# A fused decoder trunk on one core: gathered expert sums enter the output by products with 0-1 matrices, and the last three V tiles are used whole

## The chip, the cores and the metric

One core of a Trainium2 chip. The metric is the device time of one launch in microseconds (us), the median of several runs.

## The reference

Four residual layers over 256 tokens of width 1024, all in float32: an attention and retention mixer, a PEER layer, a short-convolution mixer ("odd mixer"), a second PEER layer, and a final RMSNorm. The change lies in the two PEER layers and in what follows each:

```
def peer(xn, w_q, sub_keys, u, v):        # 16384 experts, 8 heads, top 16: 128 experts for a token
    ...                                   # scores, top-k, gate (softmax), eidx
    hid = gelu(einsum('td,thkd->thk', tc, u[ec]))
    return einsum('thk,thkd->td', gc * hid, v[ec])

h = h + peer(rmsnorm(h, norm_ffn[layer]), ...)
...
return rmsnorm(h, final_norm)
```

## The kernel before

**Two ways through PEER.** The first 96 tokens (`TG`) are *gathered*: for each of 96 steps a row of `u`, later of `v`, is fetched for each of 128 partitions by an indirect transfer of 512 KB on GpSimd's queue. Partitions 0 to 95 hold one token each, with 96 of its 128 experts; partitions 96 to 127 work off the other 32 experts of tokens 0 to 31, then 32 to 63, then 64 to 95 (`SUB` = 32). The other 160 tokens (`TD`) are *dense*: all of `u` and `v` stream through as 128 tiles of 512 KB each (the U stage and the V stage), by eight buffers (`RAW`), on the queues of SyncE and, for odd V tiles, ScalarE.

**The V stage.** Eight PSUM tiles `vo[b]`, one for 128 of the 1024 output columns, hold the output transposed (columns on partitions, tokens along the free axis). Tiles in `SPL` are split: ScalarE rounds the tile to `vhi` (L1415), VectorE forms the bf16 rest `vlo` (L1422); the hidden values are split likewise (`row_parts`, `row_rest`, L1486 to L1494), and TensorE takes a product of 320 columns (L1539) and one of 160 (L1541) for each b. The other tiles are used whole, in a float32 product of 160 columns (L1504). `carry` does the splitting three tiles ahead, so that it stands that early in the instruction streams.

**The gather in the V stage.** `ga.step()` is called for every tile and adds `ga.rate` to a credit; each whole credit consumes one fetched row (`consume`, L1038: acc = row x weight + acc on VectorE) and issues the next row into the freed one of six buffers. The own tokens' sum runs on from `acc[0]` to `acc[2]`; the partial sums of partitions 96 to 127 start anew at each third and are copied by `part` (L1049, 128 KB) to the tokens' partitions of `acc[0]`. After the last step two folds (L1045) add `acc[2]` and `acc[0]` to the residual `h`. The rate is set so that the last step falls at tile 121.

**The last blocks.** `END` = 3 tiles are kept for the end, where the loop over b is outside: TensorE finishes block b for all three tiles, then ScalarE copies it out of PSUM (L1555), VectorE adds the second half of the split products (L1556), and the next norm's operand is formed. In layer 0 (`Folded`) a product with the identity puts h of the gathered tokens into the block first (L1566); the operand `x2` of the odd mixer is scaled by ScalarE and VectorE (L538, L539), and `st.parts()` splits the mixer's weight tiles 0 and 1 into the buffers `hi` and `lo`, at the start and at block 3. In layer 1 (`Final`) `fetched` normalises the gathered tokens' rows on its own and sends them out (L587 to L598); the blocks hold the dense tokens alone, squares and scaled blocks are formed (L625, L626), transposed back (L637), and scaled by the root (L663 to L669).

**The streams.** All is emitted in a written order (a manual schedule), one in-order stream for each engine. `hi` and `lo` have three buffers each, used by U's prefetch, V's splits and the mixers' splits in turn; in the mixers `st.deep` names the tiles that take two further ones. The odd mixer reads its weights in threes per k: the first pair at L280, the others at L263.

Of the kernel before, what the change touches and what calls it, by code (L numbers as in the profile page):

```python
# [15 lines left out]
OP = mybir.AluOpType  # L16
# [30 lines left out]
SPL = [i for i in range(NK) if i % 2 or i % 4 == 0 and i > 0]  # L47
# [6 lines left out]
END = 3  # L54
# [8 lines left out]
C_N = C_ONE + 1  # L63
# [7 lines left out]
def shape_constants():  # L71
# [3 lines left out]
    c[:, C_ONE] = 1.0  # L75
    c[:, C_ST:C_ST + TK] = np.array(STARTS)[None, :]
# [29 lines left out]
class Stream:  # L106
# [31 lines left out]
    def _split(self):  # L138
# [5 lines left out]
        pools = self.more if i < self.end and (self.end - i) % 5 in self.deeper else (self.hi_pool, self.lo_pool)  # L144
# [52 lines left out]
def trunk_kernel(ctx, tc, x, small, cst, mcst, ew_in, ew_out, ow_in, ow_out, wq, keys, pu, pv, pun, gains, out):  # L197
# [139 lines left out]
    Z = pers.tile([P, S], BF16, tag="z", name="z")  # L337
# [175 lines left out]
    class Folded(Norm):  # L513


        def begin(self, XT, fold):

            st.parts()
            new_x2()
            self.XT = XT  # L520
            self.fq = {}
            self.fold = fold

        def block(self, b, pend):
# [4 lines left out]
            if b == 3:  # L529
                st.parts()  # L530
# [42 lines left out]
    class Final(Sums):  # L573
# [4 lines left out]
        def __init__(self, g):  # L578
            super().__init__()
            self.g = g  # L580
            self.junk = Xb.rearrange("p k t -> p (k t)")[:, :512]

        def warm(self):
            nc.sync.dma_start(self.g, gains[2])
            self.table()

        def fetched(self):  # L587

            rows = slice(0, TG)
            for ch in range(2):  # L590
                act.activation(self.junk, h[:, 0, ch * 512:(ch + 1) * 512], AF.Square,
                               accum_out=self.w[:, 0, ch:ch + 1])
            self.mean0(0)
            self.root(0)
            self.rstd(0)
            v.scalar_tensor_tensor(h[rows, 0, :], h[rows, 0, :], self.scale(0)[rows], self.g[rows],
                                   op0=OP.mult, op1=OP.mult)
            nc.sync.dma_start(out[0, rows, :], h[rows, 0, :])  # L598

        def begin(self, XT, fold):  # L600
# [9 lines left out]
            v.memset(self.GX[:, :, :TG], 0.0)  # L610
            v.memset(self.SQ, 1.0)
# [8 lines left out]
        def ready(self, b):  # L620

            xt = self.XT[:, b, TG:]
            gain = G[:, 7 * ND + b:7 * ND + b + 1]
            sq = self.SQ[:, 1 if b else 0, TG:]
            act.activation(sq, xt, AF.Square)  # L625
            v.tensor_scalar(self.GX[:, b, TG:], xt, gain, None, op0=OP.mult)  # L626
# [1009 lines left out]
```

## Time and profile before

| | |
|---|---|
| median of 3 runs | 1510.13 us (1510.12 to 1511.16) |
| the profiled execution | 1510.24 us, span 1508.4 us |
| TensorE busy | 1442.8 us, 96% |
| VectorE, ScalarE, GpSimd busy | 1255.6, 762.1, 726.3 us |
| moved by DMA | 533 MB, mean 353 GB/s |
| granted TensorE clock, mean | 0.99 |

The span runs from the first to the last instruction; the profiled execution's time has 1.8 us around it. Times in rows count from the span's start. V's stages end near 749 us (layer 0) and 1490 us (layer 1). Idle time of an engine is of interest only where others wait for it, so what is read below are stretches, and who waits for whom at their ends.

### The profile page before, as it was taken

The numbers are of one execution on the slowest core, as the hardware profiler recorded it, in microseconds if no ns is written. First come the engines' busy times: TensorE is split into PE (matmuls) and PEld (weight loads), VectorE is DVE, ScalarE is ACT, GpSimd is POOL, SyncE is SP. The second block draws the span as 40 slices with busy tenths as digits, with TensorE's granted clock in tenths as the row PEclk, the third lists the DMA queues.
The fourth block names the chain that finished last, engine by engine and source line by source line (L and its number), as shares of the span: only waits on it lengthen the run. The fifth ranks groups of instructions, "written<-read, shape, count | busy, mean of one in ns | idle before, by whom it ended". The sixth has DMA issues, their size and how long they took to land.

```text
span 1508.4 us, 30116 instructions
## 1 busy us (share of the span) xinstructions
PE 1442.8 (96%) x11180; PEld 1338.8 (89%) x11180; DVE 1255.6 (83%) x2480; ACT 762.1 (51%) x1821; POOL 726.3 (48%) x514
## 2 busy tenths in 40 slices
PE   9999999999999999989899999999999999998896
PEld 5667999999999998888789799999999999988885
DVE  5637999879998888888866599996999978888887
ACT  5556512268875444444553462113888744444444
POOL 6754545446675343444145373453666724444430
PEclk9999999999999999999999999999999999999997
DMA  8646899999999999999956488999999999999993
GB/s 317 197 153 205 292 401 409 396 409 403 407 403 408 404 401 409 408 399 409 362 189 190 166 294 327 408 408 396 408 405 405 403 397 400 408 408 399 409 408 114
DMA packets 147442, 533.00 MB, mean 353 GB/s; under 512 B 16992, under 2 KB 17248, under 8 KB 147296
## 3 DMA queue, kind: packets, MB, share of 16 engines
q1 hardware_dynamic: 71872, 258.11, 45.6%
q0 software_dynamic: 56704, 205.07, 34.5%
q10 hardware_dynamic: 18720, 67.90, 11.4%
q8 instruction: 88, 1.44, 0.4%
q14 instruction: 58, 0.48, 0.1%
HBM read 528.34 MB, written 1.05 MB: 351 GB/s over the span
## 4 chain that ended last, share of the span: by engine, by line
PE 53%; DMA 29%; DVE 9%; issue 5%; ACT 3%; POOL 1%; ACTq 0%; SPq 0%; DVEq 0%; POOLq 0%
PE hid L1404 28%; DMA raw<-pv 18%; PE hid L263 4%; PE vo L1539 3%; DMA raw<-pu 2%; DMA rows<-pv,ig 2%; PE hid L269 2%; PE vo L1504 2%; DMA rows<-pun,ig 2%; PE G L1364 2%; PE ea L297 2%; PE ea L296 2%; PE ea L295 2%; DMA grow<-pun,ig 2%; DVE vlo L1422 1%
## 5 line engine op out<-in xcount | busy, mean ns | idle before, releaser
L1404 PE MATMUL hid<-xf,raw 128*128 128x160 f32 x3392 | 486.3, 301 | 7.2 <-DMA raw<-pu 4.5
L1404 PEld LDWEIGHTS hid<-xf,raw 128*128 128x128 f32 x3392 | 466.9, 191 | 9.6 <-issue 5.3
L1415 ACT CAST vhi<-raw 128x1024 fp32r<-128x1024 f32 x190 | 198.6, 1045 | 271.0 <-DMA raw<-pv 211.3
L1539 PE MATMUL vo<-ko,vhi 128*128 128x320 f32 x1488 | 265.9, 321 | 31.5 <-DVE ko L1494 31.2
L1422 DVE TENSOR_TENSOR vlo<-raw,vhi 128x1024 bf16<-128x1024 f32 x190 | 231.9, 1222 | 76.2 <-ACT vhi L1415 70.8
L1013 POOL DMA_INDIRECT rows<-pv,ig x128 | 184.6, 1442 | 207.6 <-DVE gacc L1038 173.6
L1539 PEld LDWEIGHTS vo<-ko,vhi 128*128 128x128 f32 x1488 | 220.6, 189 | 40.5 <-DVE ko L1494 40.1
L1013 POOL DMA_INDIRECT rows<-pun,ig x128 | 169.7, 1326 | 135.6 <-DVE rows L1023 63.6
L149 POOL TENSOR_TENSOR lo<-raw,hi 128x1024 bf16<-128x1024 f32 x70 | 168.0, 2413 | 82.5 <-ACT hi L147 78.8
L1023 DVE SCALAR_TENSOR_TENSOR rows<-rows,xg 128x1024 f32<-128x1024 f32 x128 | 155.0, 1216 | 21.5 <-DMA rows<-pun,ig 21.3
L1437 ACT ACTIVATE hg<-hid 128x160 f32<-128x160 f32 (+14 forms) x240 | 62.7, 264 | 216.9 <-PE hid L1404 214.5
L1038 DVE SCALAR_TENSOR_TENSOR gacc<-rows,ghid,gacc 128x1024 f32<-128x1024 f32 x124 | 158.4, 1278 | 5.2 <-DMA rows<-pv,ig 4.7
L1504 PE MATMUL vo<-hg,raw 128*128 128x160 f32 x1056 | 161.7, 304 | 0.7 <-DVE hg L1440 0.7
L1504 PEld LDWEIGHTS vo<-hg,raw 128*128 128x128 f32 x1056 | 147.5, 192 | 1.1 <-DVE hg L1440 1.0
L1013 POOL DMA_INDIRECT grow<-pv,ig x64 | 92.7, 1448 | 113.7 <-DVE gacc L1038 94.3
L1541 PE MATMUL vo<-hb,vlo 128*128 128x160 bf16 x1488 | 135.8, 234 | 0.0
L1013 POOL DMA_INDIRECT grow<-pun,ig x64 | 80.9, 1264 | 77.5 <-DVE grow L1023 44.0
L1354 ACT ACTIVATE ko<-ko,idxT 128x128 f16<-128x128 f16 x320 | 101.6, 391 | 29.3 <-DVE ko L1340 29.1
L1541 PEld LDWEIGHTS <-vlo 128*128 128x128 bf16 x1488 | 98.8, 98 | 19.2 <-DVE vlo L1422 0.3
L147 ACT CAST hi<-raw 128x1024 fp32r<-128x1024 f32 x100 | 102.5, 1047 | 20.2 <-issue 10.1
L263 PE MATMUL hid<-x,hi 128*128 128x256 f32 x800 | 108.5, 289 | 3.5 <-DVE cg L954 2.5
L263 PEld LDWEIGHTS hid<-x,hi 128*128 128x128 f32 x800 | 99.6, 192 | 4.4 <-ACT hi L147 2.7
(264 smaller groups left out, 2136.3 us busy)
## 6 DMA issues: line engine op xcount, KB each, us to landing
raw<-pu SPq DMA_DIRECT2D x212, 512.0 KB, 8.0
raw<-pv SPq DMA_DIRECT2D x128, 512.0 KB, 8.9
raw<-pv ACTq DMA_DIRECT2D x128, 512.0 KB, 8.6
raw<-wq SPq DMA_DIRECT2D x32, 512.0 KB, 4.1
raw<-ew_in SPq DMA_DIRECT2D x28, 512.0 KB, 4.7
raw<-ow_in SPq DMA_DIRECT2D x24, 512.0 KB, 4.5
hg<-pu SPq DMA_DIRECT2D x22, 512.0 KB, 5.5
raw<-ew_out SPq DMA_DIRECT2D x8, 512.0 KB, 3.6
```

Of the source, the lines that this page charges most:

```text
L147: self.nc.scalar.copy(hi, t)
L149: eng.tensor_tensor(lo, t, hi.bitcast(F32), OP.subtract)
L263: pe.matmul(ps[:, :S], hi[:, k * P:(k + 1) * P], A2[:, k, s_, :], start=k == 0 and s_ == 0, stop=False)
L1013: gp.indirect_dma_start(self.row(s_), None, table, bass.IndirectOffsetOnAxis(IG[:, 0, s_ % STEPS:s_ % STEPS + 1].bitcast(U32), 0))
L1023: v.scalar_tensor_tensor(r, r, 1.0, XG[:, q % 2, :], op0=OP.mult, op1=OP.mult, accum_out=w)
L1038: v.scalar_tensor_tensor(self.acc[q], r, w, self.acc[q], op0=OP.mult, op1=OP.add)
L1404: pe.matmul(ps[:, :TD], w[k], XF[:, k, :], start=k == 0, stop=k == ND - 1)
L1415: act.copy(whi[j], raw)
L1422: v.tensor_tensor(wlo[j], raw, whi[j].bitcast(F32), OP.subtract)
L1504: pe.matmul(vo[b][:, TG:S], w[:, c], HG[:, i, :], stop=i == NK - 1, **m)
L1539: pe.matmul(vo[b][:, TG:S + TD], hi[:, b * P:(b + 1) * P], hs, **m)
L1541: pe.matmul(vo[b][:, TG:S], lo[:, b * P:(b + 1) * P], hb, **m)
```

## The change

Each third of the gather now begins its accumulator anew for all 128 partitions (`acc[q]`, no copies, no folds). The sums leave by TensorE: `leave(b, q)` multiplies block b of `acc[q]` with a constant 128 x 96 matrix of zeros and ones (`C_M`, in the constants), which puts a token's own sum and the sum of the partition that helped it into the same column of `vo[b]`. The sets for q = 0 and 1 follow two steps after their third, inside the V loop; the set for q = 2 opens each of the last blocks. The identity products take all 128 tokens of h's first half (before 32). V tiles 125 to 127 are whole. The gather's rate divides by 2 tiles more, so that the last step falls at tile 123. In layer 1 the gathered tokens pass through the last blocks like the others: 256 columns there, no norm of their own, no gains loaded, and all output leaves at the end by four transfers of 256 KB on SyncE's queue. In layer 0 the odd mixer's tiles 0 and 1 are split ahead of the last blocks and tile 2 at block 5, and other tiles of the mixer take the further buffers. The warm-up operand `Z` lies in `Xb` instead of a tile of its own.

The diff, cut:

```
+END = 3
+SPL = [i for i in range(NK - END) if i % 2 or i % 4 == 0 and i > 0]
...
+C_N = C_M + 3 * TG
...
+    for q in range(3):
+        for t in range(TG):
+            c[t, C_M + q * TG + t] = 1.0
+            if t // SUB == q:
+                c[TG + t % SUB, C_M + q * TG + t] = 1.0
...
-    Z = pers.tile([P, S], BF16, tag="z", name="z")
+    Z = Xb[:, 0, :]
...
         def begin(self, XT, fold):                      # Folded; the first st.parts() stays
+            st.parts()
...
-            if b == 3:
+            if b == 5:
                 st.parts()
...
         def warm(self):                                 # Final
-            nc.sync.dma_start(self.g, gains[2])
             self.table()
-        def fetched(self):
...
-            xt = self.XT[:, b, TG:]
+            xt = self.XT[:, b, :]
...
+            for n, (th, ch) in enumerate(((1, 0), (1, 1), (0, 0), (0, 1))):
+                o = self.put[:, ch] if th else h[:, 0, ch * 512:(ch + 1) * 512]
...
+                nc.sync.dma_start(out[th, :, ch * 512:(ch + 1) * 512], o)
...
-            st.deep(mp2, 4 * ND, (1, 2))
+            st.deep(mp2, 4 * ND, [4 * ND - k for k in (3, 4, 8, 9, 13, 14, 19, 20, 25, 26, 30, 31)])
...
-            elif j == 0:
-                v.tensor_scalar(self.acc[0], r, w, None, op0=OP.mult)
             elif j % SUB == 0:
-                v.scalar_tensor_tensor(self.acc[q][:TG], r[:TG], w[:TG], self.acc[q - 1][:TG], op0=OP.mult, op1=OP.add)
-                v.tensor_scalar(self.acc[q][TG:], r[TG:], w[TG:], None, op0=OP.mult)
-                self.part(q - 1)
+                v.tensor_scalar(self.acc[q], r, w, None, op0=OP.mult)
...
-            ga.rate = (ga.TOTAL - ga.c) / (NK - 8.5)
+            ga.rate = (ga.TOTAL - ga.c) / (NK - 6.5)
...
+            def leave(b, q):
+                pe.matmul(vo[b][:, :TG], ga.acc[q][:, b * P:(b + 1) * P], C[:, C_M + q * TG:C_M + (q + 1) * TG],
+                          start=False, stop=False, skip_group_check=True)
...
-                    pe.matmul(vo[b][:, TG:P], h[:, 0, c], ident[:, TG:], **m)
+                    pe.matmul(vo[b][:, :P], h[:, 0, c], ident, **m)
...
-                if i == NK - 6:
-                    assert ga.c == ga.TOTAL
-                    ga.fold(2)
-                if i == NK - 5:
-                    ga.fold(0)
-                if i == NK - 4 and last:
-                    norm.fetched()
+                while sent < 2 and ga.c > STEPS + (sent + 1) * SUB + 1:
+                    for b in range(ND):
+                        leave(b, sent)
+                    sent += 1
...
             for b in range(ND):
-                if not last:
-                    pe.matmul(vo[b][:, :TG], h[:, 0, b * P:(b + 1) * P], ident[:, :TG], start=False, stop=False,
-                              skip_group_check=True)
+                leave(b, 2)
                 for n, w in enumerate(ws):
                     products(b, NK - END + n, w)
```

How the instructions move is shown at three places. First TensorE's first last block in layer 0 (`vo` the block, `h` the residual, `gacc` the accumulator, `ko` and `vhi` the rounded, `hb` and `vlo` the low parts, `hg` and `raw` the whole ones), before:

```order
L1541 LDWEIGHTS vlo_7576
L1541 MATMUL vo_4966<-hb_7528,vlo_7576 128x160
L1566 MATMUL vo_4959<-cst,h 128x96
L1507 MATMUL vo_4959<-ko_4967,vhi_7574 128x320
L1508 LDWEIGHTS vlo_7589
L1508 MATMUL vo_4959<-hb_7528,vlo_7589 128x160
L1504 MATMUL vo_4959<-hg_1256,raw_7507 128x160
L1507 MATMUL vo_4959<-ko_4967,vhi_7610 128x320
L1508 LDWEIGHTS vlo_7633
L1508 MATMUL vo_4959<-hb_7612,vlo_7633 128x160
```

and now:

```order
L1517 MATMUL vo_4965<-hb_7538,vlo_7583 128x160
L1493 MATMUL vo_4958<-cst,gacc_1259 128x96
L1475 MATMUL vo_4958<-hg_1255,raw_7504 128x160
L1475 MATMUL vo_4958<-hg_1255,raw_7517 128x160
L1475 MATMUL vo_4958<-hg_1255,raw_7541 128x160
L1493 MATMUL vo_4959<-cst,gacc_1259 128x96
```

The first product of a block reads the accumulator instead of h, and three whole products stand where five of both kinds stood.

Second, VectorE at the end of layer 1's V stage (`nw` the norm's small columns, `fin` the last blocks' tile), before, where rows of the small norm chain are left out between the two pieces:

```order
L1038 SCALAR_TENSOR_TENSOR gacc_8857<-rows_9645,ghid_8858,gacc_8857 128x1024
L1422 TENSOR_TENSOR vlo_15172<-raw_15068,vhi_15147 128x1024
L1045 TENSOR_TENSOR h<-gacc_8857,h 96x1024
L1422 TENSOR_TENSOR vlo_15183<-raw_15092,vhi_15170 128x1024
L1045 TENSOR_TENSOR h<-gacc_8855,h 96x1024
```

```order
L596 SCALAR_TENSOR_TENSOR h<-h,nw_8849,xf 96x1024
L1422 TENSOR_TENSOR vlo_15234<-raw_15129,vhi_15202 128x1024
L1494 TENSOR_TENSOR ko_12560<-hg_8853,ko_12560 128x160
L610 MEMSET fin_15237 128x8x96
L611 MEMSET fin_15237 128x512
```

and now:

```order
L1393 TENSOR_TENSOR vlo_15139<-raw_15035,vhi_15113 128x1024
L1465 TENSOR_TENSOR ko_12540<-hg_8833,ko_12540 128x2x160
L1018 SCALAR_TENSOR_TENSOR gacc_8837<-rows_9625,ghid_8838,gacc_8837 128x1024
L1393 TENSOR_TENSOR vlo_15159<-raw_15059,vhi_15137 128x1024
L1018 SCALAR_TENSOR_TENSOR gacc_8837<-rows_9625,ghid_8838,gacc_8837 128x1024
L1529 TENSOR_TENSOR xg<-vo_12532,xg 128x160
L611 TENSOR_SCALAR fin_15202<-xg,small 128x256
L1529 TENSOR_TENSOR xg<-vo_12533,xg 128x160
```

Between the last accumulation and the first block's add nothing is left; the last accumulation itself now stands behind the low half of tile 124 instead of ahead of it.

Third, ScalarE around the start of layer 0's last blocks (`hi` the mixer's rounded weights, `xg` the copied blocks, `x` the scaled ones), before:

```order
L1415 CAST vhi_7610<-raw_7531 128x1024
L1486 CAST ko_4967<-hg_1256 128x160
L1487 CAST hb_7612<-hg_1256 128x160
L147 CAST hi_7644<-raw_7554 128x1024
L1555 COPY xg<-vo_4959 128x256
L1555 COPY xg<-vo_4960 128x256
L538 ACTIVATE x_7650<-xg,small 128x256
L1555 COPY xg<-vo_4961 128x256
L538 ACTIVATE x_7650<-xg,small 128x256
L1555 COPY xg<-vo_4962 128x256
L538 ACTIVATE x_7650<-xg,small 128x256
L147 CAST hi_7690<-raw_7578 128x1024
```

and now:

```order
L1386 CAST vhi_7559<-raw_7481 128x1024
L153 CAST hi_7640<-raw_7564 128x1024
L153 CAST hi_7647<-raw_7585 128x1024
L1528 COPY xg<-vo_4958 128x256
L1528 COPY xg<-vo_4959 128x256
L545 ACTIVATE x_7646<-xg,small 128x256
L1528 COPY xg<-vo_4960 128x256
L545 ACTIVATE x_7646<-xg,small 128x256
L1528 COPY xg<-vo_4961 128x256
```

The rounding of the mixer's tiles 0 and 1 stands ahead of the first copy; before, tile 1 stood between the copies of blocks 3 and 4.

## Rows read from the trace of the kernel before

**Rows 1.** The busy time of each engine in six stretches (core 0). Columns: the stretch, its length, busy time (count) of PE, PEld, DVE, ACT and POOL, granted TensorE clock (1.00 is 2.4 GHz), DMA share, GB/s. The first four lie around the end of layer 0's V stage and in the odd mixer, the fifth in layer 1's V stage, the last in layer 1's last blocks.

```profile
748.70:752.40 3.70, 0.04 (x1) 0.00 (x1) 1.28 (x2) 1.14 (x2) 0.00 (x0) 1.00 0.97 333
752.40:755.80 3.40, 3.40 (x15) 2.90 (x15) 2.78 (x4) 0.37 (x1) 0.00 (x0) 0.50 0.47 137
762.30:769.70 7.40, 6.50 (x51) 5.89 (x50) 6.47 (x12) 6.23 (x16) 2.21 (x3) 1.00 0.48 142
792.70:797.00 4.30, 4.25 (x23) 3.92 (x24) 3.02 (x5) 0.20 (x1) 1.81 (x1) 0.60 0.69 217
1430.00:1455.00 25.00, 22.11 (x186) 20.53 (x184) 20.78 (x20) 12.09 (x15) 10.76 (x8) 1.00 1.03 408
1490.30:1496.30 6.00, 6.00 (x24) 4.66 (x25) 3.84 (x11) 2.18 (x7) 0.00 (x0) 0.50 0.11 36
```

**Rows 2.** The timeline of TensorE from the end of layer 0's V stage into the odd mixer: start, length, engine, line, operation, out<-in, shapes, count; in brackets the idle time before and what ended it. A product of two float32 operands counts as x2.

```profile
748.02 0.73 PE L1541 MATMUL vo<-hb,vlo 128*128 128x160 bf16 x8
752.40 0.74 PE L1566 MATMUL vo<-cst,h 128*128 128x96 f32 x2 [3.66 <-DVE h L1045]
...
757.17 0.40 PE L1566 MATMUL vo<-cst,h 128*128 128x96 f32 x2
757.35 0.39 PE L1507 MATMUL vo<-ko,vhi 128*128 128x320 f32 x1
...
762.33 0.36 PE L280 MATMUL hid<-x,hi 128*128 128x256 f32 x1
...
769.73 1.91 PE L285 MATMUL hid<-xb,lo 128*128 128x256 bf16 x16
...
787.24 2.15 PE L263 MATMUL hid<-x,hi 128*128 128x256 f32 x16 [1.04 <-DVE u L956]
...
792.75 3.27 PE L263 MATMUL hid<-x,hi 128*128 128x256 f32 x16 [2.47 <-DVE cg L954]
```

**Rows 3.** The timeline of VectorE (the second fold of layer 0) and of GpSimd (the issue of layer 0's last gathered row), columns as before.

```profile
751.12 1.22 DVE L1045 TENSOR_TENSOR h<-gacc,h 96x1024 f32<-96x1024 f32 x1 [2.44 <-DMA gacc<-gacc]
...
725.82 0.94 POOL L1013 DMA_INDIRECT rows<-pv,ig  x1 [0.65 <-DVE gacc L1038]
```

**Rows 4.** The timeline of ScalarE in layer 0's last blocks: the split of the odd mixer's tile 1, a copy of a block out of PSUM, and the scaling of a block by the norm's gain.

```profile
761.94 1.05 ACT L147 CAST hi<-raw 128x1024 fp32r<-128x1024 f32 x1 [2.75 <-PE vo L1507]
...
764.93 0.35 ACT L1555 COPY xg<-vo 128x256 f32<-128x256 f32 x1
765.26 0.51 ACT L538 ACTIVATE x<-xg,small 128x256 fp32r<-128x256 f32 x1
```

**Rows 5.** The timeline of TensorE at the end of layer 1's V stage: a whole tile, two split tiles, the first product after the wait, and two transposes with the product behind them.

```profile
1462.29 2.38 PE L1504 MATMUL vo<-hg,raw 128*128 128x160 f32 x16
1464.40 1.44 PE L1539 MATMUL vo<-ko,vhi 128*128 128x320 f32 x8
...
1466.20 1.42 PE L1539 MATMUL vo<-ko,vhi 128*128 128x320 f32 x8
...
1490.29 0.61 PE L1507 MATMUL vo<-ko,vhi 128*128 128x320 f32 x1 [6.02 <-DVE ko L1494]
...
1498.96 0.38 PE L637 MATMUL fq<-cst,fin 128*128 128x128 f32 x2
1499.10 0.39 PE L1507 MATMUL vo<-ko,vhi 128*128 128x320 f32 x1
```

**Rows 6.** The timeline of VectorE there: the last accumulation of a gathered row, the first fold, the low half of the last split tile, and the two steps of a last block that lie on its scaled operand and its squares.

```profile
1478.97 1.28 DVE L1038 SCALAR_TENSOR_TENSOR gacc<-rows,ghid,gacc 128x1024 f32<-128x1024 f32 x1
...
1481.31 1.21 DVE L1045 TENSOR_TENSOR h<-gacc,h 96x1024 f32<-96x1024 f32 x1
...
1489.83 0.32 DVE L1494 TENSOR_TENSOR ko<-hg,ko 128x160 fp32r<-128x160 f32 x1
...
1498.85 0.30 DVE L626 TENSOR_SCALAR fin<-xg,small 128x160 f32<-128x160 f32 x1
1499.21 0.33 DVE L628 TENSOR_TENSOR fin<-fin 128x160 f32<-128x160 f32 x1
```

**Rows 7.** The timeline of ScalarE in the last blocks (copies out of PSUM, a square), and of the queue of SyncE with the last issue of the program.

```profile
1499.16 0.29 ACT L1555 COPY xg<-vo 128x160 f32<-128x160 f32 x1
...
1500.16 0.29 ACT L1555 COPY xg<-vo 128x160 f32<-128x160 f32 x1
1500.84 0.34 ACT L625 ACTIVATE fin<-xg 128x160 f32<-128x160 f32 x1 [0.39 <-DVE xg L1556]
...
1505.13 0.33 SPq L669 DMA_DIRECT2D out<-h  x1
```

**Rows 8.** The issue of layer 1's last gathered row on GpSimd; the DMA queues between 1460 and 1465 us (q0 is the gather's, q1 SyncE's, q10 ScalarE's: packets, MB, share of 16 engines) and the time from issue to landing of the row issued in that stretch; the same time for the two rows issued between 720 and 730 us.

```profile
1460.19 0.93 POOL L1013 DMA_INDIRECT rows<-pv,ig  x1 [0.66 <-DVE gacc L1038]
...
q10 hardware_dynamic: 208, 0.78, 39.0%
q0 software_dynamic: 195, 0.71, 35.6%
q1 hardware_dynamic: 156, 0.56, 28.2%
...
rows<-pv,ig POOLq DMA_INDIRECT x1, 18.6
...
rows<-pv,ig POOLq DMA_INDIRECT x2, 14.8
```

More of the change, by code (lines that the diff above doesn't have):

```diff
@@ L46 @@
 UPTO = (112, 110)
-SPL = [i for i in range(NK) if i % 2 or i % 4 == 0 and i > 0]
+END = 3
+SPL = [i for i in range(NK - END) if i % 2 or i % 4 == 0 and i > 0]
 CODE = 64.0
@@ L62 @@
 C_ONE = C_IB + TK
-C_N = C_ONE + 1
+C_M = C_ONE + 1
+C_N = C_M + 3 * TG
 M_COS = 0
@@ L143, in _split @@
         t = self.raw.pop(i)
-        pools = self.more if i < self.end and (self.end - i) % 5 in self.deeper else (self.hi_pool, self.lo_pool)
+        pools = self.more if i < self.end and self.end - i in self.deeper else (self.hi_pool, self.lo_pool)
         hi = pools[0].tile([P, D], F32R, tag="hi", name=f"hi{i}")
@@ L620, in ready @@
         def ready(self, b):
-            xt = self.XT[:, b, TG:]
+            xt = self.XT[:, b, :]
             gain = G[:, 7 * ND + b:7 * ND + b + 1]
-            sq = self.SQ[:, 1 if b else 0, TG:]
+            sq = self.SQ[:, 1 if b else 0, :]
             act.activation(sq, xt, AF.Square)
-            v.tensor_scalar(self.GX[:, b, TG:], xt, gain, None, op0=OP.mult)
+            v.tensor_scalar(self.GX[:, b, :], xt, gain, None, op0=OP.mult)
             if 0 < b < ND - 1:
-                v.tensor_tensor(self.SQ[:, 0, TG:], self.SQ[:, 0, TG:], sq, OP.add)
+                v.tensor_tensor(self.SQ[:, 0, :], self.SQ[:, 0, :], sq, OP.add)
         def back(self, b):
@@ L722, in even_mixer @@
         with tc.tile_pool(name=nm("mix"), bufs=1) as mp, tc.tile_pool(name=nm("mix2"), bufs=2) as mp2:
-            st.deep(mp2, 4 * len(GORD) + ND, (2, 3))
+            st.deep(mp2, 4 * len(GORD) + ND, [k for k in range(40) if k % 5 in (2, 3)])
             M = mp.tile([P, M_N], F32, tag="mcst", name="mcst")
@@ L1544, in peer @@
                     ga.step()
-                if i == NK - 6:
-                    assert ga.c == ga.TOTAL
-                    ga.fold(2)
-                if i == NK - 5:
-                    ga.fold(0)
-                if i == NK - 4 and last:
-                    norm.fetched()
+                while sent < 2 and ga.c > STEPS + (sent + 1) * SUB + 1:
+                    for b in range(ND):
+                        leave(b, sent)
+                    sent += 1
+            assert ga.c == ga.TOTAL and sent == 2
             def fold(b):
-                t = slice(TG if last else 0, S)
-                act.copy(XT[:, b, t], vo[b][:, t])
+                act.copy(XT[:, b, :], vo[b][:, :S])
                 v.tensor_tensor(XT[:, b, TG:], vo[b][:, S:S + TD], XT[:, b, TG:], OP.add)
@@ L1596, in trunk_kernel @@
         odd_mixer(b, a)
[L1597 removed]
+        peer(1, a, Final())
 def kernel(**inputs):
@@ L1626 @@
         "pun": ct(a["peer_u"].reshape(2 * NK * P, D)),
-        "gains": ct(np.broadcast_to(gains[[1, 3, 4], None, :], (3, P, D))),
+        "gains": ct(np.broadcast_to(gains[[1, 3], None, :], (2, P, D))),
     }
```

42 lines of the change are left out of this document (7 added, 35 removed).

## The prediction

> **What bounds the kernel now.** I read the windows first. In the middle of layer 1's V stage the DMA share is 1.03 at 408 GB/s while TensorE works 22.11 of 25 us [rows 1]: the transfers set the pace there, so only bytes count, and TensorE has 12% to spare. The chain of waits then leads to two places where no transfer is the limit. In layer 0 TensorE ends the last streamed block at about 748.7 and next starts at 752.40; the row names the fold of the sums into h (L1045), a wait of 3.66 us [rows 2], and that fold waited 2.44 us itself for the copy of 32 partitions [rows 3]. In layer 1 the wait is 6.02 us, until 1490.29, on the low half of the last split tile (L1494) [rows 5]. That half is late because VectorE stands in order behind two folds and the separate norm of the gathered tokens: folds from 1481.31, the half only at 1489.83 [rows 6]. Both times TensorE comes back at a granted clock of 0.50, that is 1.2 GHz, for 3.4 us and 6 us [rows 1]. A third place follows layer 0's wait: the products of the odd mixer's first two tiles take 7.40 us of which TensorE works 6.50 [rows 1], and ScalarE could not split tile 1 before 761.94, since the buffer it writes was still read by the last V blocks (2.75 us, L1507) [rows 4].
>
> **The change part by part.** All sums stand against the profiled execution's own 1510.24 us (span 1508.4); the median of the runs is 0.1 us from it.
>
> *Start of the last blocks, layer 0.* Folds and copies are gone. The first product of the last blocks now waits for the last accumulation; behind it on TensorE is everything that remains of the stage, and the two first splits of the odd mixer stand behind that accumulation on VectorE. The slower rate moves the issue of the last gathered row from the step of V tile 112 to that of tile 114, later by the 3.9 us that one whole and one split tile take (1462.29 to 1466.20) [rows 5]. It was issued at 725.82 [rows 3]; landing takes 14.8 us there and 18.6 us in layer 1 [rows 8]. Two of the three copies (128 KB, 0.3 us each at 408 GB/s) leave the saturated stretch before it: 725.82 + 3.9 - 0.6 + (14.8 to 18.6) = 743.9 to 747.7, and 1.28 for the accumulation [rows 6] makes 745.2 to 749.0. TensorE itself is free at 748.7 - 0.6 = 748.1. I take 748.6 instead of 752.40: **3.8 us**.
>
> *The last blocks, layer 0.* Before, 752.40 to 762.33, 9.9 us. At full clock the five blocks from 757.17 on take 1.03 each [rows 2]. After: one product with a 0-1 matrix per block, of the shape of L1566, 0.18 us (757.17 to 757.35) [rows 2], and three whole products of 2.11/8 = 0.26 (1462.29 to 1464.40) [rows 5]: 0.97. So fewer instructions, but hardly less TensorE time; the gain is the clock. 8 x 0.97 + 0.2 = 8.0: **1.9 us**. ScalarE needs 0.35 and 0.51 per block [rows 4] and stays under 0.97; the third split (1.05 of ScalarE [rows 4], 1.2 of VectorE) now falls into block 5 and delays the mixer's last operand to an estimated 2.5 us behind the last block (the rest of that split, and a copy, an add and a scaling). The mixer's products take 0.6 us per k and 0.8 for the transposes between, so they reach the eighth operand about 4.7 us after they start: covered.
>
> *Into the mixer.* Three splits are ready, into buffers free since V's tile 124, so the 7.40 - 6.50 = **0.9 us** of stalls go [rows 1].
>
> *Stalls further in.* TensorE waits 1.04 and 2.47 us for VectorE at 787.24 and 792.75, then runs that tile at a clock of 0.60, 3.27 us against 2.15 for the same 16 products [rows 1, 2], 1.1 us more: 4.6 in all. After the change one split less stands between the first two results of the mixer on ScalarE (one cast, 1.05). The other buffers change which split waits for whom; no row shows that. Bounds: all 4.6 gained, or one split late and 1.0 lost. I take **1.5**, nearest to the one cast.
>
> *Start of the last blocks, layer 1.* Last row: 1460.19 [rows 8] + 3.9 - 0.6 + 18.6 + 1.28 = 1483.4. But 512 KB for gains (1.3 us at 408 GB/s) no longer pass ahead of the end, so 1482.1. TensorE, free at about 1483.0 before, comes to 1481.1 with the same bytes gone. I take 1482.0 instead of 1490.29: **8.3 us**. Bounds 1480.5 and 1484.2.
>
> The Trainium skill ("DMA: Bandwidth & Descriptors", Queues, rings and completion order) says that each DMA engine goes round the queues that have work. By it the gather queue gets a third, six rows of 0.5 MB need 23.1 us, and this start would be 5.9 us later. The rows lean the same way: with three queues busy the gather queue had 35.6% [rows 8], yet its row landed in 18.6, as V's queues empty by the end.
>
> *The last blocks, layer 1.* Before, 1490.29 to the last square's end at 1501.18, 10.9 us; the full-clock pace was 1.00 (copies 1499.16, 1500.16) [rows 7]. After, TensorE has 3 x 0.26 + 0.18 and two transposes of 0.14 to 0.38 together [rows 5]: 1.19. ScalarE and VectorE now do 256 columns where they did 160: the cycle copy, add, square grows from 1.00 to about 1.18 by scaling the copy (0.29) and the square (0.34) [rows 7], as VectorE's does by its two steps of 0.30 and 0.33 [rows 6]. So 1.0 for block 0, 7 x 1.19, and 1.3 to the last square's end: 10.6, **0.3 us**. It is no longer the matter of a half clock.
>
> *The output.* The first 96 rows no longer leave early; after the last scaling 1.05 MB go instead of 0.66. The last issue is at 1505.13 [rows 7]. Between 0 and 0.39 MB / 408 GB/s = 1.0 lost; I take **-0.4**, since the four transfers start one after the other.
>
> *Elsewhere.* The constants grow by 147 KB right ahead of the first weights on their queue: 0 to 0.4 lost (147 KB at 408 GB/s), **-0.3** taken. The two early sets of products (16 of 0.18, 2.9 us a layer) and the wider identity products (under 0.1 each, 8 a layer) lie in the DMA-bound stretch with its 12% of slack; without that cover both layers would lose 3.7 us each, 7.4 in all. The warm-up operand in another tile: nothing.
>
> **Sum:** 3.8 + 1.9 + 0.9 + 1.5 + 8.3 + 0.3 - 0.4 - 0.3 = 16.0. 1510.24 - 16.0 gives **1494 us**.
>
> **The rivals.**
> *The gathered rows become the new wait.* By the queue's 35.6% of 408 GB/s (145 GB/s), six rows take 21.7 us: the starts move to 752.1 and 1486.5, 3.5 and 4.5 later: **1502 us**. For it: every row of the gather waits over 14 us, and V's later tiles stop making room for it. Against: by 740 to 750 the old gather was through, and the total bytes are fewer. The Trainium skill's round of queues, above, would add some 1.4 us in each layer. Chance 0.15.
> *The mixer gives layer 0's gain back.* ScalarE and VectorE carry the same splits and norm as before, and waits of 1.04 and 2.47 already name VectorE. If they only start after the old interval, the 6.6 + 1.5 are lost: **1502 us**. Against: most of ScalarE's delay is the 2.75 wait that goes. Chance 0.10; with the first rival together, about 1508, 0.04.
> *All early mixer stalls go*, clock included: 3.1 more, **1491 us**. Chance 0.15.
> *The half clock, and slower.* In place: the last blocks of both layers, where TensorE now waits a little in each block for the other engines. If it ran at 1.2 GHz there, layer 0's blocks would cost 0.97 more each (7.8), the 6.5 of the mixer's first products 3.4 and the third tile 1.5 (by 3.27 / 2.15), the mixer gain of 1.5 would be lost, and layer 1's blocks would take 2.38 instead of 1.19 (9.5): 23.7 more, **1518 us**. It decides against the change from about 16 of these 23.7 us on. For it: 0.50 stands in both places today [rows 1]. Against: each low stretch follows a wait of 2.47 us or more [rows 2, 5]; with 0.9 us of small gaps between 762.3 and 769.7 the clock stayed at 1.00 [rows 1]. The Trainium skill ("TensorE: Matmul & The Clock Gate", A second HAM failure mode: psum-queue depth-cycling) reports the clock swinging from frequent small idles alone; the stretch just named does not show it. Chance 0.03.
>
> **How the numbers follow.** Forecast 1494: 0.53, its own range 1489 to 1498.5. Faster by over 0.2% (about what a measurement of this kernel tells from no change) means under 1507: forecast, both single rivals and the better mixer, 0.93. Within 0.2%: both rivals together, 0.04. Slower: the half clock, 0.03. The range 1486.5 to 1502.5 holds the forecast with its bounds, both single rivals' values, and 1491 with starts 1.5 earlier in both layers and the mixer gain 1 larger; both together and the clock stay outside.
>
> **What would show it.** Right: no wait over 1.5 us ahead of the last blocks in either layer, granted clock near 1.00 in them, block paces near 0.97 and 1.19, layer 0's low products of the mixer's first pair (L285 before) some 6.6 us earlier, the span's end about 18.2 us after layer 1's first last-block product (10.6, and the 7.2 from 1501.18 to 1508.4 with 0.4). Wrong: a wait on the accumulation of several us, or on ScalarE or VectorE in the mixer's first three tiles; a V stage whose DMA share falls below 1; a clock of 0.50 in the blocks.

## The result and the profile after

The changed kernel takes **1490.72 us** (median of 4 runs, 1490.64 to 1491.80) against 1510.41 of the kernel before on the same chip (1510.12 to 1511.16): ratio **0.9871**, 95% interval 0.9853 to 0.9888. The profiled span fell from 1508.4 to 1488.7 us. The forecast was 1494 in a range of 1486.5 to 1502.5: the side is right and the time lies 3.3 us under the forecast; by parts, the profiled spans give a gain of 19.7 where the sum had 16.0.

First the windows of the profile after, in the columns of [rows 1]: layer 0's last blocks, the mixer's first pair, a stretch in the middle of the mixer, the middle of layer 1's V stage, layer 1's last blocks.

```profile
746.20:754.40 8.20, 8.20 (x66) 8.20 (x65) 6.77 (x14) 6.33 (x14) 1.22 (x2) 1.00 0.67 253
754.40:761.70 7.30, 7.30 (x66) 7.12 (x65) 4.34 (x11) 6.41 (x17) 3.98 (x3) 1.00 0.80 293
801.90:811.30 9.40, 7.42 (x50) 6.53 (x49) 7.12 (x10) 3.84 (x5) 5.36 (x3) 0.82 0.36 114
1430.00:1455.00 25.00, 23.67 (x198) 22.03 (x197) 21.39 (x21) 12.08 (x15) 12.27 (x8) 1.00 1.02 408
1470.00:1480.60 10.60, 10.57 (x85) 10.27 (x82) 7.62 (x22) 5.77 (x16) 0.00 (x0) 1.00 0.01 2
```

In both last blocks TensorE works without a gap at a granted clock of 1.00; before, both began at 0.50 [rows 1]. V still moves 408 GB/s. The stretch with idle TensorE and a clock of 0.82 is a new one, inside the mixer.

TensorE from layer 0's last split tile into the mixer, after (columns as in [rows 2]):

```profile
745.60 0.73 PE L1517 MATMUL vo<-hb,vlo 128*128 128x160 bf16 x8
746.16 0.40 PE L1493 MATMUL vo<-cst,gacc 128*128 128x96 f32 x2
746.40 1.01 PE L1475 MATMUL vo<-hg,raw 128*128 128x160 f32 x6
747.24 0.36 PE L1493 MATMUL vo<-cst,gacc 128*128 128x96 f32 x2
...
753.47 0.36 PE L1493 MATMUL vo<-cst,gacc 128*128 128x96 f32 x2
753.67 1.01 PE L1475 MATMUL vo<-hg,raw 128*128 128x160 f32 x6
754.40 2.18 PE L286 MATMUL hid<-x,hi 128*128 128x256 f32 x16
...
760.08 1.91 PE L291 MATMUL hid<-xb,lo 128*128 128x256 bf16 x16
```

No row has a bracket: the product with the 0-1 matrix (L1493) starts where the split tile ends. A block takes 1.04 us, and the mixer's first pair goes from 754.40 to its low products in 5.68 us instead of 7.40.

VectorE's last accumulation and the split behind it, and GpSimd's issue of layer 0's last gathered row, after (they answer to [rows 3]):

```profile
744.52 1.28 DVE L1018 SCALAR_TENSOR_TENSOR gacc<-rows,ghid,gacc 128x1024 f32<-128x1024 f32 x1
745.71 1.22 DVE L155 TENSOR_TENSOR lo<-raw,hi 128x1024 bf16<-128x1024 f32 x1
...
727.04 1.68 POOL L997 DMA_INDIRECT rows<-pv,ig  x1 [1.22 <-DVE gacc L1018]
```

The accumulation ends at 745.80, beside TensorE's last split tile and only 0.4 us ahead of the product that reads it. Layer 1, TensorE again, beside [rows 5], and VectorE's last accumulation there, which ends at 1469.53, 0.5 us ahead:

```profile
1468.21 1.42 PE L1515 MATMUL vo<-ko,vhi 128*128 128x320 f32 x8
1469.47 0.73 PE L1517 MATMUL vo<-hb,vlo 128*128 128x160 bf16 x8
1470.03 0.40 PE L1493 MATMUL vo<-cst,gacc 128*128 128x96 f32 x2
...
1476.75 0.38 PE L622 MATMUL fq<-cst,fin 128*128 128x128 f32 x2
1476.97 0.36 PE L1493 MATMUL vo<-cst,gacc 128*128 128x96 f32 x2
1477.16 1.01 PE L1475 MATMUL vo<-hg,raw 128*128 128x160 f32 x6
1478.01 0.38 PE L622 MATMUL fq<-cst,fin 128*128 128x128 f32 x2
...
1468.25 1.28 DVE L1018 SCALAR_TENSOR_TENSOR gacc<-rows,ghid,gacc 128x1024 f32<-128x1024 f32 x1
```

The wait of 6.02 us is gone. A block with transposes takes 1478.01 - 1476.75 = 1.26 us, and TensorE is what fills it.

Now the odd mixer, after: first TensorE, then VectorE, then ScalarE. `cg` and `z` are products that VectorE forms out of TensorE's results.

```profile
779.61 2.14 PE L269 MATMUL hid<-x,hi 128*128 128x256 f32 x16 [0.41 <-DVE cg L938]
...
801.15 1.05 PE L275 MATMUL hid<-xb,lo 128*128 128x256 bf16 x8
804.18 2.66 PE L269 MATMUL hid<-x,hi 128*128 128x256 f32 x16 [1.98 <-DVE z L951]
806.64 1.93 PE L275 MATMUL hid<-xb,lo 128*128 128x256 bf16 x8
...
827.04 2.15 PE L269 MATMUL hid<-x,hi 128*128 128x256 f32 x16 [1.48 <-DVE cg L938]
```

```profile
802.46 1.22 DVE L155 TENSOR_TENSOR lo<-raw,hi 128x1024 bf16<-128x1024 f32 x1 [3.83 <-ACT hi L153]
803.61 0.42 DVE L951 TENSOR_TENSOR z<-hid,y 128x256 f32<-128x256 f32 x1
```

```profile
801.38 1.04 ACT L153 CAST hi<-raw 128x1024 fp32r<-128x1024 f32 x1 [7.13 <-issue]
...
821.96 1.05 ACT L153 CAST hi<-raw 128x1024 fp32r<-128x1024 f32 x1 [7.12 <-issue]
```

Of the early stalls [rows 2] 0.41 us is left. But two casts now stand over 7 us, VectorE stands behind them in order, and TensorE waits for what VectorE makes next (`z` the first time, `cg` the second).

**Where the 19.7 us came from**, between the same points of TensorE's stream in both profiles: start of layer 0's last blocks 6.2 (752.40 to 746.16), those blocks 1.7, the first pair 1.7: a lead of 9.65 us. At the mixer's tenth tile it is 14.7 (797.08 to 782.40), at its second half 9.1 (838.98 to 829.84): the mixer as a whole gives 0.5 back. Layer 1's start of the last blocks 11.1 more (1490.29 to 1470.03 is 20.26), the blocks 0.3, the tail from the last square to the end -0.8. These are differences of two profiles. In the kernels below that leave a V stage as it is, that stage varies by some 1.6 us from profile to profile (254.5 to 256.1 us in layer 0, 256.4 to 257.9 in layer 1), so a term is good to a us or two.

### The profile page after: what moved, and what is told of

It reads as the page before. It is cut to its first block, busy times and chain, and to the rows that moved or that the text cites. A ratio compares the mean times of both kernels' runs of the same rounds, so it can differ in the third digit from the quotient of the medians.

```text
span 1488.7 us, 30208 instructions
## 1 busy us (share of the span) xinstructions
PE 1443.5 (97%) x11260; PEld 1345.4 (90%) x11260; DVE 1239.5 (83%) x2457; ACT 755.8 (51%) x1808; POOL 735.8 (49%) x508
## 4 chain that ended last, share of the span: by engine, by line
PE 57%; DMA 23%; DVE 13%; issue 3%; ACT 3%; POOL 0%; ACTq 0%; SPq 0%; DVEq 0%; POOLq 0%
PE hid L1375 27%; DMA raw<-pv 19%; PE vo L1515 5%; PE vo L1475 4%; PE hid L269 3%; PE G L1335 2%; PE vo L1517 2%; PE ea L303 2%; PE ea L302 2%; PE ea L301 2%; PE hid L275 2%; DMA raw<-pu 1%; ACT vhi L1386 1%; DVE rows L1007 1%; DVE hg L1114 1%
## 5 line engine op out<-in xcount | busy, mean ns | idle before, releaser
L1386 ACT CAST vhi<-raw 128x1024 fp32r<-128x1024 f32 x186 | 194.5, 1046 | 263.6 <-DMA raw<-pv 192.8
L997 POOL DMA_INDIRECT rows<-pv,ig x128 | 190.2, 1486 | 216.0 <-DVE gacc L1018 184.5
L1393 DVE TENSOR_TENSOR vlo<-raw,vhi 128x1024 bf16<-128x1024 f32 x186 | 227.4, 1223 | 82.8 <-ACT vhi L1386 66.1
L1475 PE MATMUL vo<-hg,raw 128*128 128x160 f32 x1120 | 168.7, 302 | 1.0 <-DVE hg L1411 0.9
L1475 PEld LDWEIGHTS vo<-hg,raw 128*128 128x128 f32 x1120 | 154.7, 190 | 1.5 <-DVE hg L1411 1.5
L997 POOL DMA_INDIRECT grow<-pv,ig x64 | 95.7, 1496 | 108.0 <-DVE gacc L1018 95.0
L997 POOL DMA_INDIRECT grow<-pun,ig x64 | 84.5, 1321 | 74.9 <-DVE grow L1007 46.3
```

Source lines behind the costliest of these rows:

```text
L997: gp.indirect_dma_start(self.row(s_), None, table, bass.IndirectOffsetOnAxis(IG[:, 0, s_ % STEPS:s_ % STEPS + 1].bitcast(U32), 0))
L1386: act.copy(whi[j], raw)
L1393: v.tensor_tensor(wlo[j], raw, whi[j].bitcast(F32), OP.subtract)
L1475: pe.matmul(vo[b][:, TG:S], w[:, c], HG[:, i, :], stop=i == NK - 1, **m)
```

## The experiments

Twelve kernels, all made from the changed one. They ran in four groups beside the kernel before, so the ratios to it are compared; the interval of each is 0.0013 to 0.0017 to either side, 2 to 2.6 us, so that a difference between two of them is uncertain by some 3 us. Each row shown is from one execution.

| changed kernel, but | us | ratio |
|---|---|---|
| as it is | 1490.72 | 0.9871 |
| third buffer in the mixer's second pool | 1485.89 | 0.9833 |
| late list | 1485.64 | 0.9835 |
| old list | 1488.69 | 0.9851 |
| old split times | 1494.39 | 0.9892 |
| old gather rate | 1491.67 | 0.9868 |
| narrow copies back | 1496.51 | 0.9897 |
| the same bytes from 128 partitions | 1492.53 | 0.9879 |
| one load of gains back | 1490.78 | 0.9872 |
| four such loads | 1494.96 | 0.9903 |
| tiles 125, 127 split | 1502.40 | 0.9941 |
| 125, 127 split and old split times | 1500.68 | 0.9932 |
| late list and two output queues | 1486.03 | 0.9832 |

**What stalls the mixer.** Tiles are split into two pools, of three and of two buffers; the list names those of the second. Counted from the mixer's first, the cast at 801.38 is tile 18, the one at 821.96 tile 24. Tiles 15 to 18 and 21 to 24 are four in a row in the pool of three.

```
third buffer: - st.deep(mp2, ..., k in (3,4,8,9,13,14,      19,20,      25,26,30,31))
              + st.deep(dp,  ..., k in (3,4,8,9,13,14,18,19,20,24,25,26,30,31))   # dp: bufs=3
late list:    + st.deep(mp2, ..., k in (3,4,8,9,13,14,18,19,23,24,30,31))
old list:     + st.deep(mp2, 4 * ND, [k for k in range(40) if k % 5 in (1, 2)])
```

> The changed kernel with a third buffer in the second pool of split tiles of the odd mixer (and tiles 18 and 24 sent to that pool, so that no more than three tiles in a row take the first pool's three buffers). Theory: the stalls at 801.95 (2.2 us, then 1.6 for the slower clock) and at 825.3 (1.7) come from tiles 18 and 24, each the fourth in a row in a pool of three: their casts stood 7.1 us on ScalarE until tiles 15 and 21 were through, and VectorE stood behind them. Then both stalls go, the mixer's second half starts near 824.3 instead of 829.84, and the time is about 1485.2 us. Rival, the weights land late or VectorE has too much work there: both stalls stay, 1490 to 1491 us. Second rival, the next shortage takes what is won: the second half starts near 824 to 827 and the time is 1487 to 1489.

> The changed kernel with the second pool's tiles moved: 18, 19, 23, 24 instead of 19, 20, 25, 26, so that the row of more than three tiles in the first pool is 25 to 29, in the mixer's second half, where no product waits for VectorE. No buffer is added. Theory of the fourth tile in a row: the stalls at 801.95 and 825.3 go, the casts of 28 and 29 wait instead, but TensorE needs these only three tiles (8 us) later: about 1485.2 us. Rival, weights or VectorE's load: 1490 to 1491 us with both stalls in place.

> The changed kernel with the odd mixer's second-pool tiles as they were before (0, 1, 5, 6, 10, 11 and so on); tiles 0 to 2 are split before that pool is there, so tiles 0 to 4 take the first pool. Theory: the fourth and fifth of these five wait, and the early stalls near TensorE's tiles 7 to 10 come back, 3.5 to 4.6 us, while the rest of the list has no four in a row and the stalls at 801.95 and 825.3 (5.5 us) go: 1488.5 to 1491 us with the stalls in the mixer's first third. Rival, the list does not matter: 1490.7 with stalls where they are now. Rival, the early stalls were ended by the early splits alone: 1485.2.

Both new lists gave what the theory asks, 1485.9 and 1485.6. With the late list, which adds no buffer, the mixer up to its second half took 69.9 us (755.78 to 825.68) instead of 75.4, the clock never fell, and the only long wait of a cast is in the second half, where no product of TensorE waits for it. ScalarE, then TensorE's first product of the second half:

```profile
802.26 2.00 ACT L153 CAST hi<-raw 128x1024 fp32r<-128x1024 f32 x2
805.56 1.05 ACT L153 CAST hi<-raw 128x1024 fp32r<-128x1024 f32 x1 [1.29 <-issue]
...
831.32 1.05 ACT L153 CAST hi<-raw 128x1024 fp32r<-128x1024 f32 x1 [3.81 <-PE acc L302]
```

```profile
825.68 0.48 PE L301 MATMUL acc<-hi,c2o 128*128 128x512 f32 x1
```

This is shown, then: a tile that is fourth in a pool of three stalls ScalarE, and behind it VectorE and TensorE where TensorE still needs what VectorE makes. The late list is also the best version run: 0.9835 (0.9821 to 0.9848), some 5 us under the changed kernel.

The old list fell in its range too (1488.5 to 1491): the two stalls went, and an early one came back. TensorE, then ScalarE:

```profile
783.05 2.15 PE L269 MATMUL hid<-x,hi 128*128 128x256 f32 x16 [1.44 <-DVE cg L938]
```

```profile
760.55 1.05 ACT L153 CAST hi<-raw 128x1024 fp32r<-128x1024 f32 x1 [2.15 <-PE hid L286]
```

So the new list, as written, costs some 3 us by itself. The times alone (0.9871 beside 0.9851) hardly clear their uncertainty; the mixer up to its second half does show it, 72.1 us (755.68 to 827.74) instead of 75.4. The list moves the shortage from tile 3, the fourth of five in a row there, to 18 and 24.

**Whole tiles and early splits.** Four kernels make a square.

```
old split times:  - st.parts()  (second one in Folded.begin);  - if b == 5:   + if b == 3:
125, 127 split:   - SPL = [i for i in range(NK - END) ...]     + SPL = [i for i in range(NK) ...]
```

> The changed kernel with the splits ahead of the odd mixer as before: one before the last blocks and one in block 3, the new list kept. Theory, the early splits end the early stalls: the low products of the mixer's first pair come 0.5 to 1 us later and the stalls near TensorE's tiles 8 and 10 come back in part, 1492 to 1495 us. Rival, the new list ended them: 1490.7 to 1491.5 us. Rival, a later start of the first tiles only shortens the stalls at 801.95 and 825.3: 1488 to 1490.5.

> The changed kernel with V's tiles 125 and 127 split again, as before; the sums still leave by products. It tells what the whole tiles are worth by themselves. Theory: at full clock a block takes as long either way (1.03 before, 1.04 now), but two casts, two low halves and the low half of the weights' partner return to ScalarE and VectorE beside the last accumulation and the mixer's first splits: the last blocks wait 1 to 2.5 us for VectorE in each layer and the mixer's first splits come later, 1493 to 1497 us. Rival, the wait before was the folds and the norm alone, and the low halves are ready in time now: 1490.3 to 1491.5.

> The changed kernel with V's tiles 125 and 127 split as before and also the odd mixer's early splits as before (one ahead of the last blocks, one in block 3). With the split tiles alone it took 1502.4 us: the mixer's second split stood 10.3 us on ScalarE for the buffer of V's last split tile, and with it all eight copies of the blocks. Theory, this blocking is most of the cost, and the split tiles alone cost the wait for the low half (1.6 us), the half clock after it (2 us) and the later mixer: 1495 to 1498.5 us. Rival, the split tiles themselves cost it: 1501 to 1503 us.

Whole tiles and early splits 0.9871, whole tiles alone 0.9892, early splits alone 0.9941, neither 0.9932. Old split times cost 3.2 us, in the range expected, but by one part of the theory only: one early stall is back (2.48), the two late ones stay, and the first pair's low products come no later than after the change (5.68 us behind the pair's start). The mixer up to its second half takes 77.8 us (754.89 to 832.71) instead of 75.4.

```profile
782.49 2.14 PE L269 MATMUL hid<-x,hi 128*128 128x256 f32 x16 [2.48 <-DVE cg L937]
...
807.06 2.73 PE L269 MATMUL hid<-x,hi 128*128 128x256 f32 x16 [1.98 <-DVE z L950]
...
829.92 2.14 PE L269 MATMUL hid<-x,hi 128*128 128x256 f32 x16 [1.48 <-DVE cg L937]
```

Split ends cost 10.6 us where I had expected 2 to 6. TensorE, ScalarE and the window of the last blocks in that run (layer 0); the profile is of the slowest of its five executions, 1506.82 us, 4.4 over the median:

```profile
750.82 0.64 PE L1478 MATMUL vo<-ko,vhi 128*128 128x320 f32 x1 [1.57 <-DVE ko L1465]
...
764.13 1.10 PE L286 MATMUL hid<-x,hi 128*128 128x256 f32 x3 [2.54 <-ACT x L545]
```

```profile
761.00 1.05 ACT L153 CAST hi<-raw 128x1024 fp32r<-128x1024 f32 x1 [10.33 <-PE vo L1478]
```

```profile
748.20:757.00 8.80, 7.22 (x31) 5.89 (x31) 2.62 (x3) 2.44 (x4) 0.00 (x0) 0.62 0.68 229
```

The wait on the low half (L1465) returns, with a clock of 0.62 behind it; and the mixer's second split, issued ahead of the blocks, waits for the buffer of V's last split tile, with all eight copies of the blocks behind it on ScalarE. My theory for the run with both made that blocking most of the cost, 1495 to 1498.5; it fell. Without the early split it is still 1500.68, the rival's 1501 to 1503 within the interval. Beside its own partner, the whole tiles with old split times, it is (0.9932 - 0.9892) x 1510 = 6.0 us: that is the price of the split tiles without the long blocking. TensorE, ScalarE and VectorE there:

```profile
750.83 0.63 PE L1477 MATMUL vo<-ko,vhi 128*128 128x320 f32 x1 [1.76 <-DVE ko L1464]
...
1481.50 0.46 PE L1492 MATMUL vo<-cst,gacc 128*128 128x96 f32 x2 [0.77 <-DVE gacc L1017]
```

```profile
748.24 1.05 ACT L1385 CAST vhi<-raw 128x1024 fp32r<-128x1024 f32 x1 [3.68 <-DMA raw<-pv]
...
760.91 1.05 ACT L153 CAST hi<-raw 128x1024 fp32r<-128x1024 f32 x1 [2.75 <-PE vo L1477]
...
749.32 1.23 DVE L1392 TENSOR_TENSOR vlo<-raw,vhi 128x1024 bf16<-128x1024 f32 x1 [1.34 <-ACT vhi L1385]
```

These rows name the cause of the wait: V's last tile landed at about 748.2, and as a split tile it needs a cast and VectorE's low half, 2.6 us in all, before its product can start. A whole tile is used as it lands; after the change nothing waits there.

In layer 0 the products for the sums alone win little: from the first V product to the mixer's first product 271.9 us (489.39 to 761.30), against 273.7 before (488.65 to 762.33) and 265.7 after. The blocks do start 5.1 us earlier than before (258.6 us behind the first V product instead of 263.8), but then take 13.3 us (748.03 to 761.30) instead of 9.9, with that wait and the half clock behind it. In layer 1 they win almost everything: from V's first product to the last blocks 259.0 us (1222.50 to 1481.50), against 269.1 before (1221.21 to 1490.29) and 258.2 after (1211.85 to 1470.03). So the folds and the norm were layer 1's wait; how much of it was the folds and how much the norm was not separated. In layer 0 the folds hid the wait for the split tiles: both had to go. Whole tiles with the folds kept were not run, so the shares hold in this order only.

**Why V itself ended earlier.** From V's first product to its last split tile: layer 0 258.1 to 255.6 us (488.70 to 744.34 after), layer 1 260.0 to 256.4. Forecast were 0.6 and 1.9.

```
old rate:      - ga.rate = (ga.TOTAL - ga.c) / (NK - 6.5)        + / (NK - 8.5)
narrow copies: + gp.dma_start(spare[:SUB, :], ga.acc[sent][TG:, :])        # 32 x 1024, behind each leave
wide copies:   + gp.dma_start(spare[:, :D // 4], ga.acc[sent][:, :D // 4])  # 128 x 256
gains, one:    + nc.sync.dma_start(<spare>, gains[1])                       # in Final.warm
gains, four:   + if last and i in (NK-40, NK-30, NK-20, NK-10): nc.sync.dma_start(<spare>, gains[1])
```

> The changed kernel with the gather's old rate (the rest spread over NK - 8.5 steps instead of NK - 6.5). The prediction moved the last gathered row 3.9 us later by the new rate and priced that against the gain. Theory, near its end V waits for bytes and not for that row: the issue and the last accumulation come 3 to 4 us earlier than 727.04 and 744.5, the last blocks start where they do now (746.2 and 1470.0, within 1 us), 1490 to 1491.5 us. Rival, the slower rate is what lets V end earlier (2.4 us in layer 0, 3.8 more in layer 1): the starts are 2 to 4 us later, 1493 to 1497 us. Rival, the row still decides: the starts come up to 2 us earlier, 1487 to 1489.5.

> The changed kernel with two copies of 32 partitions (128 KB each) from the accumulators put back in each layer's V stage, at about their old places, into a buffer that nobody reads. It puts a price on the copies alone. Theory of the prediction, only their bytes count: 0.6 us a layer, 1491.5 to 1492.2 us. Rival, a copy keeps the transfers or GpSimd's queue, which also issues the gathered rows, for far longer than its bytes: V ends 1.5 to 2.5 us later in each layer, 1494 to 1496 us. Rival, they were hidden: 1490.3 to 1491.2.

> The changed kernel with two copies a layer as in the run with the copies put back, the same 128 KB each from one buffer on the chip to another, but from 128 partitions (256 columns) instead of 32 (1024 columns). Those cost 4 to 5 us in all, 1.1 a copy, with the DMA share at 1.03 and only 338 to 347 GB/s in their 5 us. Theory, the few partitions are what slows the transfers: 1491.3 to 1492.5 us here. Rival, a copy on the chip costs that whatever its shape: 1494.5 to 1497 us.

> The changed kernel with a load of 512 KB put back where layer 1's separate norm fetched its gains, ahead of V's last tiles, into a buffer that nobody reads. Layer 1's V stage gained 1.4 us more than layer 0's; theory, that is these bytes: 512 KB at 408 GB/s = 1.3 us, 1491.7 to 1492.4 us, the last blocks of layer 1 start 1.3 later. Rival, it was hidden: 1490.3 to 1491.2. Rival, like the copies it costs more than its bytes: 1493 us or more.

> The changed kernel with four loads of 512 KB in the last 40 tiles of layer 1's V stage, into a buffer that nobody reads: four times the bytes of the run with the gains back, which was within the spread of 2 us. Theory, in this stretch every byte moves the end by its time: 2.1 MB at 408 GB/s = 5.1 us, 1495 to 1497 us, and one load is worth 1.3 of the 3.7 us that layer 1's V stage gained. Rival, TensorE or VectorE sets the end there and the bytes are hidden in part: 1490.5 to 1493.5 us, and the 1.2 us that the copies leave unexplained in layer 1 stay unexplained.

The rate is worth nothing that can be told (0.9868 beside 0.9871), though the starts of the last blocks in that profile came 1.8 and 2.1 us later, not within 1 us as the theory had it, and the last row's issue 1.0 and 2.4 earlier instead of 3 to 4. Two narrow copies a layer lengthen V by 2.9 and 2.5 us, the whole run by (0.9897 - 0.9871) x 1510 = 3.9, as the rival had it and three times what the theory allowed; from 128 partitions the same bytes cost 1.2 by the ratios, which is no more than their own time (4 x 128 KB at 408 GB/s = 1.3) and within the interval of nothing. Windows of 5 us behind a narrow copy and behind a wide one (issued at 539.1 and 539.3), and behind the first copy of the kernel before (issued at 535.9):

```profile
545.00:550.00 5.00, 5.00 (x44) 4.80 (x43) 4.59 (x4) 2.09 (x5) 1.86 (x1) 1.00 1.03 338
```

```profile
545.00:550.00 5.00, 5.00 (x44) 4.80 (x43) 4.68 (x4) 2.09 (x5) 1.94 (x2) 1.00 1.02 405
```

```profile
540.00:545.00 5.00, 5.00 (x43) 4.80 (x42) 5.00 (x6) 1.46 (x2) 3.12 (x3) 1.00 1.04 347
```

The share of the engines is nearly the same in all three; what they move is not. All four narrow copies of that run and the two early ones in each layer of the kernel before show such a dip (338 to 371 GB/s in the lowest 5 us behind each); in the 20 us behind the four wide copies it never falls under 388. The dip is 5 us x (408 - 338) = 0.35 MB, 0.9 us, and with the copy's own 0.3 it makes 1.2 a copy, 2.4 a layer. It stood in the profile before, but I had looked at 25 us without a copy. The two shapes differ in the length of a row too (4 KB and 1 KB a partition), so that the number of partitions is the likely cause and not the only one left.

One load of gains could not be told from nothing (1490.78). Four took 1494.96, (0.9903 - 0.9871) x 1510 = 4.8 us, and put 263.4 us between V's first product and layer 1's last blocks instead of 258.2: some 1.2 each, at the lower edge of the theory's range, so bytes do count there. Copies 2.5 and gains 1.2 add up to layer 1's 3.7, but that is partly luck: the profile after has the shortest such stage of the six kernels that leave it alone (256.4 to 257.9 us), and in the run with wide copies it took 259.5, longer than with narrow ones (258.8) and without a dip behind the copies. Layer 0's 2.9 stands clear of its spread; layer 1's split between copies and gains is not shown.

**The tail.**

```
- nc.sync.dma_start(out...)     + (nc.sync if n % 2 else nc.scalar).dma_start(out...)   # and the late list
```

> The changed kernel with the late list of second-pool tiles (1485.6 us before) and with the four transfers of the output dealt out between the queues of ScalarE and SyncE instead of all on SyncE. Theory, the tail of 8.05 us from the last square to the end holds one issue behind the other on one queue: it falls by 0.3 to 0.9, 1484.7 to 1485.3 us. Rival, the tail is the bytes and the last landing: no change, 1485.6. Rival, ScalarE's own issues stand ahead of its last scaling: 0.1 to 0.5 longer.

No change (0.9832 beside 0.9835). ScalarE's last issue is at 1480.06, 4.38 behind the last square at 1475.68, and the span still ends 8.4 us behind that square, as in the changed kernel (1480.23 to 1488.7). The expected 0.3 to 0.9 lies under what the times can tell; the tail in the profile says the same. One queue was not the limit; what of the tail is landing time was not separated further.

## Why the prediction held, and where it missed

*Start of the last blocks, layer 0*: 3.8 forecast, 6.2 measured. The mechanism held; two sizes failed. "Two of the three copies (128 KB, 0.3 us each at 408 GB/s)" should have been about 1.2 each: the step took a copy for its bytes. And the last row was to be issued 3.9 later by the new rate; it was issued 1.2 later (725.82 to 727.04), as V ran 2.5 us ahead by then, and by the run with the old rate an earlier issue brings no earlier end. The last accumulation, which I let set the start at 748.6, ended at 745.80, hidden behind TensorE, but by 0.4 us only: with split ends it was what the blocks first waited for (0.77 us in layer 1, above). The sum has no term for the landing of V's last tile; with split tiles that would have taken most of the earlier start back (above).

*The last blocks, layer 0*: 1.9 forecast, 1.7 measured; the pace 1.04 where 0.97 was worked out. The clock was full, as the sum wanted, and the run with split ends shows it fall to 0.62 when the low half is waited for.

*Into the mixer*: 0.9 forecast, 1.7 measured. The 6.50 us of busy time was no floor: without gaps the same products take 5.68. The buffer wait went with the split tiles, not with the early splits: with old split times the pair still took 5.68 us (754.89 to 760.57), with split ends and old times 7.40 (761.30 to 768.70).

*Stalls further in*: 1.5 forecast, -0.5 measured. This step failed in kind. I wrote that "the other buffers change which split waits for whom; no row shows that", and bounded the loss by one split; the list could have been counted: four in a row for three buffers, twice. The early stalls nearly all went, the third rival, and gave a lead of 14.7; then 5.5 us were lost at the two tiles. 1491 came out near the result, but not by that rival's sum. That the forecast itself lies within 3.3 us is luck in part: three steps (the two starts and the mixer's first pair) gave 6.0 us more than forecast and this one 2.0 less.

*Start of the last blocks, layer 1*: 8.3 forecast, 11.1 measured: the copies 1.9 too low again, and the last accumulation once more ahead of TensorE. *Its blocks*: 0.3 and 0.3; pace 1.26 for 1.19. *Output*: -0.4 forecast, -0.8 measured. *Constants*: -0.3 forecast; not to be told: the two profiles enter layer 0's V stage within 0.1 us of each other (488.65 and 488.70), but the other kernels, the same up to there, between 489.1 and 490.6.

The gathered rows did not become the wait: the last one of layer 1 was issued at 1451.45 and accumulated from 1468.25, 16.8 us later, and no row of the stage waits for it. That rival's 4.5 us in layer 1 also left out the 1.3 of the gains that the forecast took off; with them it is 3.2. The round of queues of the Trainium skill ("DMA: Bandwidth & Descriptors", Queues, rings and completion order), by which this start would have come 5.9 us later, did not show as a delay here. The half clock stayed out of the last blocks too: TensorE had no gap in them to lose it by. The prediction's argument against that rival, that each low stretch follows a wait of 2.47 us or more, did not hold as a rule: the clock fell behind waits of 1.98 us in the mixer (0.82) and 1.57 with split ends (0.62), and stayed at 1.00 behind one of 2.48 with old split times, whose 16 products take 2.14 us as at full clock. With 125, 127 split and old split times the waits of 2.47 and 1.98 us at the mixer's same two places cost no clock either:

```profile
791.65 2.15 PE L269 MATMUL hid<-x,hi 128*128 128x256 f32 x16 [2.47 <-DVE cg L937]
...
816.22 2.15 PE L269 MATMUL hid<-x,hi 128*128 128x256 f32 x16 [1.98 <-DVE z L950]
```

The length of a single wait does not settle it, and what does was not tested. Whether the 1.1 us of clock behind the 2.47 [rows 2] come in every execution of the kernel before is open.

## What to carry to other kernels

Count a rotating pool against the list that draws on it: a tile that needs the buffer of one not yet used stops its engine's queue, and everything in order behind it. In a stage that is bound by transfers, price a copy on the chip by the throughput of the few microseconds behind it, not by its bytes. And look for what an early step must have free: the early splits paid, some 3 us, once the last V tiles had stopped holding a buffer; with split tiles they gained nothing (0.9941 beside 0.9932).

## What was new about the chip

A copy of 128 KB from 32 partitions to 32 others slowed all queues: 338 to 347 GB/s at a DMA share of 1.03 and 1.04, against 405 to 410 for the same bytes across 128 partitions; it cost about 1.0 to 1.2 us instead of 0.3. The Trainium skill ("SBUF — State Buffer", Door 1: The DMA port swizzle) says that the bandwidth of a transfer depends on how many of the memory's ports its partitions reach. The two runs agree with it in direction; that the other queues are held up as well is what the windows show: in the narrow copy's 5 us the three queues moved 0.75, 0.50 and 0.45 MB, in the wide one's 0.87, 0.60 and 0.55.

The same wait of TensorE can cost its full clock or not: behind 1.98 us at one place of the mixer 16 products took 2.66 us after the change (clock 0.82 around them), 2.73 with old split times and 2.15 with 125, 127 split and old split times; behind 2.47 us they took 3.27 before and 2.15 in that last run.
